# Sums of weight quarters: by accumulating DMAs, instead of on GpSimd, in a decoder's MLP

## The chip, the cores and the metric

The program runs on one core of a Trainium2 chip, in one launch. The metric is the device time of the launch in microseconds, the median of several runs. The engines are TensorE (PE; PEld is its weight load), VectorE (DVE), ScalarE (ACT), GpSimd (POOL) and SyncE (SP), which here only issues DMAs. Sixteen DMA engines serve the core.

## The reference

A trunk of two layers, on 512 tokens of width 1024, all in float32. Layer 0 is a stick-breaking attention, layer 1 a gated linear recurrence (HGRN2); a squared-ReLU MLP of width 4096 follows each. Only the MLP matters here.

```python
def squared_relu_mlp(h, w1, w2):
    a = jax.nn.relu(h @ w1)
    return (a * a) @ w2

def reference(...):
    for layer in range(DEPTH):
        ...
        h = rmsnorm(x, norm_gains[layer, 1])
        x = x + squared_relu_mlp(h, mlp_w1[layer], mlp_w2[layer])
    return x
```

## The kernel before

**Numbers.** A float32 product is made of three products of a shorter format: every operand is split into a rounded part (`hi`, made by ScalarE as a cast) and the rest (`lo`, made by VectorE or GpSimd as operand minus `hi`), and TensorE forms hi·hi, hi·lo and lo·hi into the same PSUM buffer. So each weight tile costs one ScalarE cast and one subtraction before TensorE can use it. The split halves of a slab of weights are `wh` and `wl`, two buffers each: while TensorE works with one slab, the next is split.

**The MLP** goes in four rounds per layer, eight in all. A round `q` takes 1024 of the 4096 hidden columns.

1. Four slabs of `mlp_w1`, 256 columns each, two chains of 24 matmuls per slab (`gemm_w`). Each chain gives 128 hidden rows for 512 tokens in PSUM (tag `mm`, two buffers). VectorE empties it into `u` (ReLU and norm factor), ScalarE squares `u`, and `Seven.take` makes from it the left operands of the second matrix. The first four chunks give A11 and A21 (`raw_a`, split as `a11`); with the last four come A12 and A22 (`a`, split as `a2h`, `a2l`) and the sums S3 and S1 (`s31h`, `s31l`), S4 and S2 (`s42h`, `s42l`).
2. The second matrix is done as a 2 x 2 block product with seven block products instead of eight (`seven_products`): A is tokens by hidden columns, cut in the middle of both; B is the 1024 x 1024 piece of `mlp_w2`, cut into quarters B11, B12, B21, B22. Each quarter is two tiles of 128 x 1024 (512 KB each), named `raw`. The right operands are B11, B21, B22 and four sums: T1 = B12 - B11, T2 = B22 - T1, T3 = B22 - B12, T4 = B21 - T2. The sums are made in place in the quarters' tiles (`minus`). A block product is two chains of 12 matmuls, one per 128 tokens. Its PSUM buffers come from tag `mm` for the first, third, fifth and seventh product, from tag `z` (two buffers) for the others.
3. Each product is added to the residual stream `xt[0]`, `xt[1]` (left and right 512 columns, four token tiles each) by `back`, on VectorE straight from PSUM. A running sum `U` of the products a11, s2 and s3 is added to three blocks of `xt` by GpSimd.

**What sets the order.** The code is written as generators; `line` deals out TensorE's work, whose order is fixed by hand. The other engines' order is chosen by a scheduler from the program's order and its own estimates; each engine then executes its instructions strictly in the order chosen, waiting at each for its operands and buffers. `Weights.next` hands TensorE a slab and at once prepares the next one of the plan: loads (`load`), then the split (`slab`). Loads of B's quarters stand in the plan between the four slabs of `mlp_w1`.

Of the kernel before, what the change touches and what calls it, by code (L numbers as in the profile page):

```python
# [13 lines left out]
ALU = mybir.AluOpType  # L14
AX = mybir.AxisListType

P = 128
D = 1024
S = 512
# [40 lines left out]
def trunk(  # L60
# [17 lines left out]
    nc = tc.nc  # L78
# [20 lines left out]
    def f(t):  # L99
        return t.bitcast(F32)  # L100
# [71 lines left out]
    rows = sb("AT", (40, P), name="rows")  # L172
# [97 lines left out]

    def quarters(w, r0):

        got = {}

        def load(i, j):
            tag = {(0, 0): "B", (1, 0): "X5", (0, 1): "R4", (1, 1): "R4"}[i, j]
            shape = (P, 10 * P) if tag == "X5" else (P, TT, SLAB)
            got[i, j] = []
            for a in range(2):
                t = sb(tag, shape, name="raw")  # L280
                t = t if tag == "X5" else t.rearrange("p t c -> p (t c)")
                t = t[:, : 2 * S].rearrange("p (k c) -> p k c", c=S)
                r = r0 + i * (D // 2) + a * 2 * P
                nc.sync.dma_start(
                    out=t, in_=w[r : r + 2 * P, j * S : (j + 1) * S].rearrange("(k p) c -> p k c", p=P)
                )
                got[i, j].append(t)

        return got, load

    def minus(eng, o, x, y):
        for a in range(2):
            eng.tensor_tensor(out=o[a], in0=x[a], in1=y[a], op=ALU.subtract)  # L293

    def seven(w, r0):

        b, load = quarters(w, r0)

        def slab(src, eng=nc.vector):
            hi = wp.tile([P, KT // 2, S], F32R, tag="wh", bufs=2, name="wh")  # L300
            lo = wp.tile([P, KT // 2, S], F32R, tag="wl", bufs=2, name="wl")
            for a in range(2):
                c = slice(2 * a, 2 * a + 2)
                nc.scalar.copy(hi[:, c, :], src[a])  # L304
                eng.tensor_tensor(out=lo[:, c, :], in0=src[a], in1=f(hi[:, c, :]), op=ALU.subtract)  # L305
            return hi, lo

        def b11():
            got = slab(b[0, 0])
            minus(nc.gpsimd, b[0, 0], b[0, 1], b[0, 0])  # L310
            minus(nc.gpsimd, b[0, 1], b[1, 1], b[0, 1])
            return got

        def t1():
            got = slab(b[0, 0])
            minus(nc.vector, b[0, 0], b[1, 1], b[0, 0])
            return got

        def t2():
            got = slab(b[0, 0])  # L320
            minus(nc.gpsimd, b[1, 0], b[1, 0], b[0, 0])
            return got

        loads = [lambda at=at: load(*at) for at in ((0, 0), (0, 1), (1, 1), (1, 0))]
# [375 lines left out]

    def back(h, t, p, eng=nc.vector):
        eng.tensor_tensor(out=xt[h][:, t, :], in0=xt[h][:, t, :], in1=p, op=ALU.add)  # L702

# [42 lines left out]
    class Seven:  # L746
# [5 lines left out]
        def take(self, u):  # L752

            A, B = slice(0, S // 2), slice(S // 2, S)
            k = len(self.raw)
            if k < 4:
# [12 lines left out]
            nc.scalar.activation(out=a, in_=u, func=AF.Square)  # L769
            nc.gpsimd.tensor_tensor(out=raw[:, B], in0=raw[:, B], in1=a[:, B], op=ALU.add)  # L770
            self.a2.append(self.two_parts(a, "Q", "a2"))
            nc.vector.tensor_tensor(out=a[:, B], in0=a[:, B], in1=raw[:, A], op=ALU.subtract)
            nc.vector.tensor_tensor(out=a[:, A], in0=a[:, A], in1=a[:, B], op=ALU.subtract)  # L773
            self.s31.append(self.two_parts(raw, "qT", "s31"))
            self.s42.append(self.two_parts(a, "Q" if k < 2 else "qT", "s42"))
# [14 lines left out]

    def seven_products(A, done):

# [11 lines left out]

        def p5(t, p):
            back(1, t, p)
            back(1, 2 + t, p)

        def p6(t, p):
            nc.vector.tensor_add(U[t], U[t], p)  # L810
            back(1, t, U[t], nc.gpsimd)

        def p3(t, p):
            back(1, t, p)
            done(1, t)

        def p7(t, p):
            nc.vector.tensor_add(U[t], U[t], p)
            back(1, 2 + t, U[t], nc.gpsimd)
            back(0, 2 + t, U[t], nc.gpsimd)  # L820
            done(1, 2 + t)

        def p4(t, p):
            back(0, 2 + t, p)
# [12 lines left out]
    def mlp(norm, nxt=None):  # L837
        task = line.spawn(norm.finish())
        rounds = FF // D
        for q in range(rounds):  # L840
# [29 lines left out]

            yield from seven_products(A, done)

# [369 lines left out]
```

## Time and profile before

| | |
|---|---|
| median of 3 runs | 1418.32 us (1418.27 to 1420.58) |
| profiled execution | 1418.27 us, its span 1416.5 us |
| TensorE busy | 1303.9 us, 92% of the span |
| VectorE, ScalarE, GpSimd busy | 1007.0, 566.1, 419.8 us |
| mean granted TensorE clock | 0.966 |
| moved by DMA | 110.67 MB |
| attention with its projection | 0 to about 317 us |
| first MLP | 317 to 711 us |
| recurrence with its projection | 711 to 1018 us |
| second MLP | 1018 to 1416 us |

A row of the profile's groups of instructions reads: line, engine, operation, output from inputs, partitions x elements of each, count, busy time in all, mean ns of one, idle time of the engine before it and what ended that. Matmuls overlap: their durations are longer than the distance from one to the next. A wait is put down to the instruction that ended last before the waiter went on, which need not be the one that was waited for.

### The profile page before, as it was taken

How to read it: one execution, taken by the hardware profiler on the slowest of the kernel's cores; microseconds unless marked ns; L12 is line 12 of the kernel's file. 1: busy time of each engine (PE TensorE's matmuls, PEld its weight loads, DVE VectorE, ACT ScalarE, POOL GpSimd, SP SyncE). 2: the span in 40 equal slices, each digit the busy share in tenths (PEclk: the TensorE clock that was granted, in tenths of full speed). 3: DMA queues.
4: the chain of work that ended last, by engine and by line, in shares of the span. 5: the costliest groups of instructions: out<-in, count | busy, mean ns of one | idle time of the engine just before them, and what ended most of it. 6: DMA issues, size and time to landing. Idle time of an engine off the chain costs nothing. (4 is left out here: it accounts for less than half of the span.)

```text
span 1416.5 us, 17879 instructions
## 1 busy us (share of the span) xinstructions
PE 1303.9 (92%) x6817; PEld 1088.8 (77%) x6817; DVE 1007.0 (71%) x1671; ACT 566.1 (40%) x943; POOL 419.8 (30%) x331
## 2 busy tenths in 40 slices
PE   8999999999798898898889999999997988988987
PEld 7988988788577676676678888888875776766765
DVE  4887687765856757757778879796667677578575
ACT  5545364444333434334343333332433333343341
POOL 1000000003624524525513223130045245255154
PEclk9999999999899999999999999999998998999998
DMA  6211123131141141240022212134211412413201
GB/s 176 91 60 53 38 90 105 47 117 61 33 146 60 60 149 30 102 130 6 14 81 65 82 60 72 55 113 149 90 60 58 137 43 69 139 31 119 74 12 49
DMA packets 91190, 110.67 MB, mean 78 GB/s; under 512 B 3832, under 2 KB 69536, under 8 KB 91104
## 3 DMA queue, kind: packets, MB, share of 16 engines
q1 hardware_dynamic: 91024, 109.22, 24.2%
q8 instruction: 54, 0.88, 0.3%
q0 software_dynamic: 80, 0.31, 0.1%
q14 instruction: 32, 0.26, 0.1%
HBM read 107.41 MB, written 2.10 MB: 77 GB/s over the span
## 5 line engine op out<-in xcount | busy, mean ns | idle before, releaser
L154 PE MATMUL ps_mm<-xh,wh 128*128 128x512 f32 x592 | 232.6, 393 | 5.9 <-DVE xt L702 5.9
L154 PE MATMUL ps_mm<-xh,wl 128*128 128x512 f32 x592 | 230.5, 389 | 0.0
L154 PE MATMUL ps_mm<-xl,wh 128*128 128x512 f32 x592 | 230.4, 389 | 0.0
L267 DVE TENSOR_TENSOR wl<-wr,wh 128x1024 fp32r<-128x1024 f32 x134 | 177.9, 1346 | 14.2 <-ACT wh L266 13.7
L266 ACT CAST wh<-wr 128x1024 fp32r<-128x1024 f32 x134 | 136.4, 1052 | 122.9 <-PE ps_mm L154 117.8
L154 PE MATMUL ps_mm<-wh,xh 128*128 128x256 f32 x592 | 173.6, 293 | 0.0
L154 PE MATMUL ps_mm<-wl,xh 128*128 128x256 f32 x592 | 167.9, 284 | 1.3 <-DVE wl L536 1.3
L304 ACT CAST wh<-raw 128x1024 fp32r<-128x1024 f32 x112 | 112.0, 1047 | 141.3 <-PE ps_mm L154 120.5
L154 PE MATMUL ps_mm<-wh,xl 128*128 128x256 f32 x592 | 167.8, 283 | 0.0
L293 POOL TENSOR_TENSOR raw<-raw 128x1024 f32<-128x1024 f32 x48 | 132.4, 2766 | 105.0 <-DVE raw L293 61.5
L154 PEld LDWEIGHTS ps_mm<-xh,wh 128*128 128x128 f32 x592 | 111.2, 188 | 30.6 <-issue 8.3
L154 PEld LDWEIGHTS ps_mm<-xh,wl 128*128 128x128 f32 x592 | 111.1, 188 | 23.5
L154 PEld LDWEIGHTS ps_mm<-xl,wh 128*128 128x128 f32 x592 | 111.2, 188 | 22.2
L764 POOL TENSOR_TENSOR raw_a<-raw_a 128x256 f32<-128x256 f32 x32 | 23.6, 739 | 352.6 <-DVE a L763 237.1
L154 PEld LDWEIGHTS ps_mm<-wh,xh 128*128 128x128 f32 x592 | 113.5, 192 | 4.2 <-issue 3.6
L154 PEld LDWEIGHTS ps_mm<-wl,xh 128*128 128x128 f32 x592 | 113.7, 192 | 2.1 <-DVE wl L536 1.5
L305 DVE TENSOR_TENSOR wl<-raw,wh 128x1024 fp32r<-128x1024 f32 x80 | 109.6, 1402 | 6.5 <-ACT wh L304 6.5
L154 PEld LDWEIGHTS ps_mm<-wh,xl 128*128 128x128 f32 x592 | 113.7, 192 | 0.0
L702 DVE TENSOR_TENSOR xt<-xt,ps_mm 128x512 f32<-128x512 f32 x128 | 85.1, 678 | 34.6 <-PE ps_mm L154 34.4
L854 DVE SCALAR_TENSOR_TENSOR u<-ps_mm,R 128x512 f32<-128x512 f32 x60 | 41.3, 688 | 90.7 <-PE ps_mm L154 90.7
L305 POOL TENSOR_TENSOR wl<-raw,wh 128x1024 fp32r<-128x1024 f32 x32 | 90.7, 2855 | 30.8 <-ACT wh L304 30.8
L154 PE MATMUL ps_mm<-wh,a 128*128 128x512 f32 x128 | 56.3, 507 | 38.9 <-ACT s42h L779 35.5
(234 smaller groups left out, 2750.3 us busy)
## 6 DMA issues: line engine op xcount, KB each, us to landing
raw<-in_mlp_w_dram SPq DMA_DIRECT2D x64, 512.0 KB, 3.6
wr<-in_mlp_w_dram SPq DMA_DIRECT2D x64, 512.0 KB, 3.8
wr<-in_hg_w_in_dram SPq DMA_DIRECT2D x32, 512.0 KB, 3.7
wr<-in_sb_w_qkv_dram SPq DMA_DIRECT2D x22, 512.0 KB, 3.7
wr<-in_sb_w_o_dram SPq DMA_DIRECT2D x8, 512.0 KB, 4.2
wr<-in_hg_w_o_dram SPq DMA_DIRECT2D x8, 512.0 KB, 3.8
xt<-in_x_dram SPq DMA_DIRECT2D x8, 256.0 KB, 6.0
out_dram<-xt SPq DMA_DIRECT2D x8, 256.0 KB, 2.0
```

The source lines that it names most:

```text
L154: nc.tensor.matmul(o, lhsT=lhsT, rhs=rhs, start=start, stop=stop, **kw)
L266: nc.scalar.copy(hi[:, c, :], raw)
L267: nc.vector.tensor_tensor(out=lo[:, c, :], in0=raw, in1=f(hi[:, c, :]), op=ALU.subtract)
L293: eng.tensor_tensor(out=o[a], in0=x[a], in1=y[a], op=ALU.subtract)
L304: nc.scalar.copy(hi[:, c, :], src[a])
L305: eng.tensor_tensor(out=lo[:, c, :], in0=src[a], in1=f(hi[:, c, :]), op=ALU.subtract)
L702: eng.tensor_tensor(out=xt[h][:, t, :], in0=xt[h][:, t, :], in1=p, op=ALU.add)
L764: nc.gpsimd.tensor_tensor(out=raw[:, A], in0=raw[:, A], in1=raw[:, B], op=ALU.subtract)
L854: nc.vector.scalar_tensor_tensor(out=u, in0=p, scalar=0.0, in1=norm.R, op0=ALU.max, op1=ALU.mult)
```

## The change

Four things change, all in the MLP.

1. A sum of two quarters is no longer a subtraction on GpSimd or VectorE. ScalarE negates the target in place (`flip`), and a DMA that GpSimd issues adds the other quarter onto it (`accum_op=ALU.add`), either from the weights in HBM or from the other quarter's tile. The tile of B12 becomes B11 - B12, that is -T1, then with B22 from HBM T2; the tile of B11 becomes T2 - B11 = T3; the tile of B21 becomes T2 - B21 = -T4. The products with -T1 and -T4 are subtracted from `xt`. That makes eight accumulating transfers of 512 KB and six negations a round.
2. All slabs are split by ScalarE and VectorE; the two that GpSimd took go to VectorE. So do the two sums per chunk in `Seven.take` that GpSimd made.
3. `U` is added to `xt` by accumulating DMAs of 256 KB, six a round, except in the last round of a layer, where VectorE does it.
4. The order of the products: a11, s1, a12, s4, s2, s3, a22 instead of a11, a12, s1, s2, s4, s3, a22. The quarters' loads come in the order B12, B11, B22, B21 instead of B11, B12, B22, B21.

```diff
+        def flip(at, plus):
+            for a in range(2):
+                nc.scalar.mul(b[at][a], b[at][a], -1.0)
+                nc.gpsimd.dma_start(out=b[at][a], in_=plus(a), accum_op=ALU.add)
...
+        def t1():
+            flip((0, 1), lambda a: rows(0, 0, a))
+            load(1, 1)
...
+        def slab_t1():
+            got = slab((0, 1))
+            for a in range(2):
+                nc.gpsimd.dma_start(out=b[0, 1][a], in_=rows(1, 1, a), accum_op=ALU.add)
+            flip((0, 0), lambda a: b[0, 1][a])
             return got
 
-        def t2():
-            got = slab(b[0, 0])
-            minus(nc.gpsimd, b[1, 0], b[1, 0], b[0, 0])
+        def slab_b21():
+            got = slab((1, 0))
+            flip((1, 0), lambda a: b[0, 1][a])
             return got
...
         slabs = [
-            b11, lambda: slab(b[1, 0], nc.gpsimd), t1, t2, lambda: slab(b[1, 1], nc.gpsimd),
-            lambda: slab(b[0, 1]), lambda: slab(b[1, 0]),
+            lambda: slab((0, 0)), slab_t1, slab_b21, lambda: slab((1, 1)), lambda: slab((0, 1)),
+            lambda: slab((0, 0)), lambda: slab((1, 0)),
         ]
-        return [("load", g) for g in loads], [("slab", g) for g in slabs]
+        return [("load", g) for g in (b12, b11, t1, b21)], [("slab", g) for g in slabs]
...
-                nc.gpsimd.tensor_tensor(out=raw[:, A], in0=raw[:, A], in1=raw[:, B], op=ALU.subtract)
+                nc.vector.tensor_tensor(out=raw[:, A], in0=raw[:, A], in1=raw[:, B], op=ALU.subtract)
...
-            nc.gpsimd.tensor_tensor(out=raw[:, B], in0=raw[:, B], in1=a[:, B], op=ALU.add)
+            nc.vector.tensor_tensor(out=raw[:, B], in0=raw[:, B], in1=a[:, B], op=ALU.add)
             self.a2.append(self.two_parts(a, "Q", "a2"))
+            self.s31.append(self.two_parts(raw, "qT", "s31"))
...
+        def add(h, t, u):
+            if last:
+                back(h, t, u)
+            else:
+                nc.gpsimd.dma_start(out=xt[h][:, t, :], in_=u, accum_op=ALU.add)
...
         def p7(t, p):
             nc.vector.tensor_add(U[t], U[t], p)
-            back(1, 2 + t, U[t], nc.gpsimd)
-            back(0, 2 + t, U[t], nc.gpsimd)
+            add(1, 2 + t, U[t])
             done(1, 2 + t)
+            add(0, 2 + t, U[t])
...
         steps = [
-            ("a11", p1), ("a12", p2), ("s1", p5), ("s2", p6), ("s4", p3), ("s3", p7), ("a22", p4),
+            ("a11", p1), ("s1", p5), ("a12", p2), ("s4", p3), ("s2", p6), ("s3", p7), ("a22", p4),
         ]
```

In the changed kernel the cast of `slab` is line 302 (before: 304), its subtraction 303 (305), the negation 294, the accumulating transfers 295 and 324, those of `U` 824, `back` 710 (702), `u` 868 (854), the halves of `two_parts` 787 and 788 (779, 780), the sums in `take` 772, 778, 781 and 782 (764, 770, 772, 773).

GpSimd in the first round, before (the rounds are alike). The numbers behind the names tell the tiles apart: `raw_3399` and `raw_3401` are the two tiles of B11, `raw_3553` and `raw_3555` of B12, `raw_3633` and `raw_3635` of B22, `raw_3735` and `raw_3737` of B21.

```order
L770 TENSOR_TENSOR raw_a_3539<-raw_a_3539,a_3674 128x256
L293 TENSOR_TENSOR raw_3399<-raw_3553,raw_3399 128x1024
L770 TENSOR_TENSOR raw_a_3547<-raw_a_3547,a_3718 128x256
L293 TENSOR_TENSOR raw_3553<-raw_3633,raw_3553 128x1024
L293 TENSOR_TENSOR raw_3401<-raw_3555,raw_3401 128x1024
L293 TENSOR_TENSOR raw_3555<-raw_3635,raw_3555 128x1024
L770 TENSOR_TENSOR raw_a_3594<-raw_a_3594,a_3776 128x256
L305 TENSOR_TENSOR wl_3838<-raw_3735,wh_3837 128x1024
L305 TENSOR_TENSOR wl_3838<-raw_3737,wh_3837 128x1024
```

GpSimd in the second round, after (`raw_4101` and `raw_4103` are the tiles of B12, `raw_4181` and `raw_4183` of B11, `raw_4367` and `raw_4369` of B21, `raw_4729` and `raw_4731` those of the third round's B12).

```order
L324 DMA raw_4101<-in_mlp_w2_dram 128x2x512
L324 DMA raw_4103<-in_mlp_w2_dram 128x2x512
L295 DMA raw_4181<-raw_4101 128x1024
L295 DMA raw_4183<-raw_4103 128x1024
L295 DMA raw_4367<-raw_4101 128x1024
L295 DMA raw_4369<-raw_4103 128x1024
L295 DMA raw_4729<-in_mlp_w2_dram 128x2x512
L295 DMA raw_4731<-in_mlp_w2_dram 128x2x512
L824 DMA xt1_100<-U_4490 128x512
L824 DMA xt1_100<-U_4506 128x512
L824 DMA xt1_100<-U_4490 128x512
L824 DMA xt0_99<-U_4490 128x512
```

The queue holds transfers only, and the next round's first pair stands ahead of this round's sums of `U`.

VectorE where the first matrix of the second round ends, before: from the `u` of the chunk that is third from the end to that of the last.

```order
L854 SCALAR_TENSOR_TENSOR u<-ps_mm,R 128x512
L305 TENSOR_TENSOR wl<-raw,wh 128x1024 x2
L780 TENSOR_TENSOR a2l<-a,a2h 128x512
L772 TENSOR_TENSOR a<-a,raw_a 128x256
L780 TENSOR_TENSOR s31l<-raw_a,s31h 128x512
L773 TENSOR_TENSOR a<-a 128x256
L854 SCALAR_TENSOR_TENSOR u<-ps_mm,R 128x512
L780 TENSOR_TENSOR s42l<-a,s42h 128x512
```

The same place after:

```order
L868 SCALAR_TENSOR_TENSOR u<-ps_mm,R 128x512
L303 TENSOR_TENSOR wl<-raw,wh 128x1024 x2
L778 TENSOR_TENSOR raw_a<-raw_a,a 128x256
L788 TENSOR_TENSOR a2l<-a,a2h 128x512
L788 TENSOR_TENSOR s31l<-raw_a,s31h 128x512
L781 TENSOR_TENSOR a<-a,raw_a 128x256
L782 TENSOR_TENSOR a<-a 128x256
L868 SCALAR_TENSOR_TENSOR u<-ps_mm,R 128x512
L788 TENSOR_TENSOR s42l<-a,s42h 128x512
```

The sum that GpSimd made stands on VectorE (L778), and `u` stands at the same place behind the chunk before it.

VectorE at the end of the same round, with what each waits for, after (DMASW is a transfer that GpSimd issued, DMAHW one that SyncE issued):

```order
L832 TENSOR_TENSOR U<-U,ps_mm 128x512 [waits DMASW1_49,DVE_49,PE_49]
L832 TENSOR_TENSOR U<-U,ps_mm 128x512 [waits DMASW2_49,DVE_49,PE_49]
L267 TENSOR_TENSOR wl<-wr,wh 128x1024 [waits DMAHW7_49,Activation_49]
L267 TENSOR_TENSOR wl<-wr,wh 128x1024 [waits DMAHW0_49,Activation_49]
L710 TENSOR_TENSOR xt_99<-xt_99,ps_mm 128x512 [waits DMASW4_49,PE_49]
L710 TENSOR_TENSOR xt_99<-xt_99,ps_mm 128x512 [waits DMASW6_49,PE_49]
```

Before, the same instructions waited for GpSimd's arithmetic or for nothing but TensorE (`[waits PE_49,Pool_49]` at the last, `[waits DVE_49,PE_49]` at `U`). Now the second sum into `U` waits until the transfer that reads `U` is done, and the last sums into `xt` until the transfers onto them have landed; the split of the next slab of `mlp_w1` (L267) stands between.

More of the change, by code (lines that the diff above doesn't have):

```diff
@@ L269, in slab_halves, with seven, rows @@
         return hi, lo, load, split
-    def quarters(w, r0):
-        got = {}
+    def seven(w, r0):
+        b = {}
+        def rows(i, j, a):
+            r = r0 + i * (D // 2) + a * 2 * P
+            return w[r : r + 2 * P, j * S : (j + 1) * S].rearrange("(k p) c -> p k c", p=P)
         def load(i, j):
@@ L282, in load, with slab @@
                 t = t[:, : 2 * S].rearrange("p (k c) -> p k c", c=S)
[L283 to L299, printed above, removed]
+                nc.sync.dma_start(out=t, in_=rows(i, j, a))
+                b[i, j].append(t)
+        def flip(at, plus):
+            for a in range(2):
+                nc.scalar.mul(b[at][a], b[at][a], -1.0)
+                nc.gpsimd.dma_start(out=b[at][a], in_=plus(a), accum_op=ALU.add)
+        def slab(at):
             hi = wp.tile([P, KT // 2, S], F32R, tag="wh", bufs=2, name="wh")
@@ L698, in head, with back @@
             outs[slot] = split_out(shared["po"])
-    def back(h, t, p, eng=nc.vector):
-        eng.tensor_tensor(out=xt[h][:, t, :], in0=xt[h][:, t, :], in1=p, op=ALU.add)
+    def back(h, t, p, op=ALU.add):
+        nc.vector.tensor_tensor(out=xt[h][:, t, :], in0=xt[h][:, t, :], in1=p, op=op)
     def chain(o, wsl, acts):
@@ L789, in part, with seven_products @@
             return [[blk(x, at + t) for x in pair] for pair in src]
-    def seven_products(A, done):
+    def seven_products(A, done, last):
         U = []
@@ L805, in p5, with p3 @@
         def p5(t, p):
+            back(1, t, p, ALU.subtract)
+            back(1, 2 + t, p, ALU.subtract)
+        def p3(t, p):
             back(1, t, p)
-            back(1, 2 + t, p)
+        def add(h, t, u):
[3 more added lines that the diff above has]
+                nc.gpsimd.dma_start(out=xt[h][:, t, :], in_=u, accum_op=ALU.add)
         def p6(t, p):
             nc.vector.tensor_add(U[t], U[t], p)
-            back(1, t, U[t], nc.gpsimd)
-        def p3(t, p):
-            back(1, t, p)
+            add(1, t, U[t])
             done(1, t)
@@ L869, in done @@
                     nxt.turn(h, LAG["x7"] if h else LAG["x"])
-            yield from seven_products(A, done)
+            yield from seven_products(A, done, q == rounds - 1)
     def hgrn(norm):
```

24 lines of the change are left out of this document (11 added, 13 removed).

## Prediction

> **What bounds the kernel now.** I read the page first, then the waits of TensorE, then one round of the MLP instruction by instruction. The first part of the page, and TensorE's waits (total us, times, longest):
>
> ```profile
> PE 1303.9 (92%) x6817; PEld 1088.8 (77%) x6817; DVE 1007.0 (71%) x1671; ACT 566.1 (40%) x943; POOL 419.8 (30%) x331
> ...
> PE ps_mm L154 <- ACT s42h L779: 35.5, 8, 4.4
> PE ps_mm L154 <- DVE wl L305: 26.9, 16, 1.8
> PE ps_mm L154 <- DVE s42l L780: 10.9, 8, 1.6
> PE ps_mm L154 <- DVE xt L702: 6.9, 7, 1.0
> ```
>
> TensorE is the bound, and its four longest waits come 7, 8 or 16 times in eight MLP rounds: they are one pattern, repeated. The timeline of TensorE in the second round (start, duration, what stood before) and the stretches' busy times (us, PE busy, its count, then PEld, DVE, ACT, POOL, the granted clock, DMA share, GB/s) give its price.
>
> ```profile
> 459.12 0.77 PE L154 MATMUL ps_mm<-wh,a 128*128 128x512 f32 x1 [4.44 <-ACT s42h L779]
> 459.69 0.63 PE L154 MATMUL ps_mm<-wl,a 128*128 128x512 f32 x1
> 467.50 0.39 PE L154 MATMUL ps_mm<-wh,a2h 128*128 128x512 f32 x1
> 473.57 0.40 PE L154 MATMUL ps_mm<-wh,s31h 128*128 128x512 f32 x1
> 479.16 0.40 PE L154 MATMUL ps_mm<-wh,s42h 128*128 128x512 f32 x1
> 497.69 0.40 PE L154 MATMUL ps_mm<-wh,s31h 128*128 128x512 f32 x1
> 503.28 0.40 PE L154 MATMUL ps_mm<-wh,a2h 128*128 128x512 f32 x1
> 509.91 0.47 PE L154 MATMUL ps_mm<-xh,wh 128*128 128x512 f32 x1 [0.99 <-DVE xt L702]
> 558.17 0.76 PE L154 MATMUL ps_mm<-wh,a 128*128 128x512 f32 x1 [4.45 <-ACT s42h L779]
> ```
> ```profile
> 411.00:455.00 44.00, 43.68 (x192) 35.83 (x192) 25.48 (x27) 15.28 (x22) 12.69 (x9) 1.00 0.27 84
> 455.00:510.00 55.00, 44.28 (x169) 33.92 (x170) 41.44 (x43) 21.17 (x26) 29.95 (x16) 0.91 0.26 86
> ```
>
> A round lasts 558.17 - 459.12 = 99.05 us. Undisturbed, its first-matrix part takes 43.7 us (192 matmuls, clock 1.00), so each of its eight chains 5.46; one product takes 503.28 - 497.69 = 5.59 us, seven 39.1. So 82.8 us of work and 16.25 us lost: 4.44 ahead of a11; 8.38 - 5.59 = 2.8 inside a11, whose matmuls start at 0.63 instead of 0.39 us each, so a wait of this length is paid again in a lower clock; 0.5 in a12; 18.53 - 11.18 = 7.35 in s2 and s4; 1.04 at the end. Who makes TensorE wait is seen on VectorE and GpSimd:
>
> ```profile
> 444.11 0.69 DVE L854 SCALAR_TENSOR_TENSOR u<-ps_mm,R 128x512 f32<-128x512 f32 x1
> ...
> 450.50 2.60 DVE L772 TENSOR_TENSOR a<-a,raw_a 128x256 f32<-128x256 f32 x1 [0.63 <-POOL raw_a L770]
> 453.03 2.87 DVE L780 TENSOR_TENSOR s31l<-raw_a,s31h 128x512 fp32r<-128x512 f32 x1
> 455.82 2.56 DVE L773 TENSOR_TENSOR a<-a 128x256 f32<-128x256 f32 x1
> 458.30 0.68 DVE L854 SCALAR_TENSOR_TENSOR u<-ps_mm,R 128x512 f32<-128x512 f32 x1
> 461.14 0.69 DVE L780 TENSOR_TENSOR s31l<-raw_a,s31h 128x512 fp32r<-128x512 f32 x1
> 461.75 0.42 DVE L772 TENSOR_TENSOR a<-a,raw_a 128x256 f32<-128x256 f32 x1
> 450.43 7.67 POOL L293 TENSOR_TENSOR raw<-raw 128x1024 f32<-128x1024 f32 x3
> 482.40 2.22 DVE L305 TENSOR_TENSOR wl<-raw,wh 128x1024 fp32r<-128x1024 f32 x1
> 485.74 1.66 DVE L780 TENSOR_TENSOR s42l<-a,s42h 128x512 fp32r<-128x512 f32 x1
> ```
>
> The same L772 takes 0.42 us alone and 2.60 while GpSimd runs its three L293; s31l 0.69 against 2.87. Behind them stands u at 458.30, which empties the PSUM buffer that a11 needs. The wait is booked on s42h, but u ended at 458.98, just before the matmul at 459.12: it is VectorE's backlog. In s2 and s4 it is the same: wl 2.22 us, s42l 1.66.
>
> **The change part by part.** First the prices: durations of a line (least/median/greatest ns), transfers with the us from issue to landing, GpSimd's own issue of one (start, duration), and two more stretches.
>
> ```profile
> L305 DVE TENSOR_TENSOR wl<-raw,wh x80: 1211/1219/2223, 345.7 to 1403.9; 128x1024 fp32r<-128x1024 f32 x80
> L304 ACT CAST wh<-raw x112: 1030/1047/1057, 344.6 to 1402.7; 128x1024 fp32r<-128x1024 f32 x112
> L779 ACT CAST a2h<-a 128x512 fp32r<-128x512 f32 x32 | 19.9, 622 | 1.0
> raw<-in_mlp_w_dram SPq DMA_DIRECT2D x64, 512.0 KB, 3.6
> out_dram<-xt SPq DMA_DIRECT2D x8, 256.0 KB, 2.0
> 2.40 0.71 POOL L206 DMA_DIRECT2D masks_i<-in_level_masks_dram  x1
> masks_i<-in_level_masks_dram POOLq DMA_DIRECT2D x1, 300.0 KB, 5.7
> 481.00:502.00 21.00, 17.42 (x66) 13.45 (x67) 15.22 (x16) 6.13 (x7) 11.16 (x5) 0.92 0.47 155
> 455.00:481.00 26.00, 19.85 (x73) 15.03 (x73) 20.10 (x23) 12.01 (x17) 12.77 (x8) 0.87 0.00 0
> ```
>
> *GpSimd's arithmetic goes.* VectorE falls back to 0.42, 0.69 and 1.22 us.
>
> *VectorE takes on,* per round, four slab halves (4 x 1.22 = 4.9) and eight 256-wide sums (8 x 0.42 = 3.4), and loses two L293 (2.4 at the undisturbed price). Its whole round becomes: eleven slabs 22 x 1.22 = 26.8; eight u 5.5; four first-half chunks 4 x 0.84; four second-half chunks 4 x 3.33 (u left out); 16 PSUM evacuations in the products at 0.69, 11.0. Sum 60 of 82.8 us. It fits on average; tight is the second half of the first matrix, four chunks with u (16.1) and two slabs (4.9), 21.0 us in four chains, 21.8 us. So I walk it in the new order. TensorE's last two chains end at 449.2 and 454.7 (410.9 + 43.7); an instruction of VectorE follows the one before by its duration less 0.08 (461.14 to 461.75), and a hop to ScalarE costs its 0.62. From u at 444.11, as now: slab one's halves to 447.1; the sum 447.5; a2l, after ScalarE has made a negation, the square and the copy, 448.5; s31l 449.1; two differences 449.9; u of the chunk before last 450.6; s42l 451.3; then the same list for that chunk: 451.6, 452.5, 453.1, 453.9, s42l 455.2; u of the last chunk 455.9. a11 needs these two buffers at 454.7 and 457.5. Then T1's halves 457.0 and 458.1 (s1 starts at 460.3), sum 458.5, xt 459.1, a2l 459.7, s31l 460.3, needed as s1's fourth operand near 462.4. Nothing waits, and the least margin is 1.6 us. So the 4.44 and the 2.8 go.
>
> *The new order* puts s1 second and s4, s2 fourth and fifth. The last s42l, late for s2 by 1.4 us now (10.9 / 8), ends about 466 for a use at 471.4. Slab by slab VectorE finishes 464.2, 470.5, 474.7, 480.4 and 485.9 for products that start at 465.9, 471.4, 477.0, 482.6 and 488.1: the 7.35 go, with 0.9 us as least margin.
>
> *ScalarE takes on* six negations per round at 1.05 (the L304 row, same shape): 6.3 us on an engine busy 21 of 55. Two stand ahead of copies that TensorE needs: those of the next round's B12 wait for their load, behind them the copies of the sixth slab. The load is issued when slab four is split (470.5), lands 3.6 us later, so the second negation ends by 475.6; the copies wait for TensorE until 477.0 anyway. Cost nothing; if the load were 2 us later, it begins to cost. SP's queue issues the same loads in another order, and each row of it has the buffer's last reader to wait for, as now.
>
> *GpSimd's queue* issues 14 accumulating transfers a round, 14 x 0.71 = 10 us against 12.7 + 30.0 us of arithmetic. What is queued behind a wait there: the six U sums behind the two transfers for the next round's B12.
>
> *The transfers themselves* are not in this trace. Eight of 512 KB and six of 256 KB a round. Their DMA time: let p be what 512 KB occupy. The stretch 481 to 502 moved 155 GB/s at a share of 0.47, 330 GB/s at full share, so a plain one takes 1.6 us: the lower end. The upper end is the row of the only transfer in GpSimd's queue, 300 KB in 5.7 us, as if all of it were occupation: 9.7 us. What does p cost? The first can start when T1's first half is split (457.0 + 0.71), and DMA is idle there now (share 0.00); the U sum that the last evacuation of xt waits for must land by 493.0, since TensorE's next first-matrix chain needs that PSUM buffer at 493.7. In these 35.2 us DMA also carries eight loads (12.8): 22.4 us are left for 8 p + 4 (p/2) = 10 p. So nothing waits up to p = 2.2; beyond, each round of the six that sum by DMA loses 10 (p - 2.2) + 2.8 us, the 2.8 again for the clock. I take p between 1.6 and 2.2, nearest to the plain row, since both are the same 16 engines and the 5.7 was taken at the start, with all first loads under way. Latency alone: two issues after U's add (486.5) make 487.9, so 5.1 us are left to land; plain 256 KB take 2.0, twice that 4.0.
>
> The Trainium skill (Collectives: The Full Stack, "The bandwidth ceiling") says that an adding transfer reads two sources through one ring and so runs at half a copy's rate, 31 / 2 GB/s per engine. An estimate from its figures is 248 GB/s over 16 engines, p = 2.1, which leaves the sum as it is. No run here shows it yet.
>
> *The last round of each layer* sums U on VectorE: six more evacuations, 4.1 us, in a stretch where it is busy 28 of 39 by the count above.
>
> **Sum.** Eight rounds lose 8 x 16.25 = 130 us. I keep 1.5 us a round for what the walk cannot see (the 0.5 us that a12 loses now, a margin of 1 us at the round's end): 12. The profiled execution was 1418.27 us (span 1416.5 and 1.8 around it), its own median 1418.32: 1418.3 - 130 + 12 = 1300.
>
> **Rivals.**
> 1. *Accumulation at half rate.* Each byte added has to be read from two places. On this trace's own rate p = 3.2; DMA is then full from 458 on, the U sums land late, VectorE stands at its U and xt instructions, and TensorE waits 10 x 1.0 + 2.8 = 12.8 us in each of six rounds: 1300 + 77 = 1377. For it: the second read must happen. Against it: SBUF sources may be quicker than the loads from which 330 GB/s comes. The Trainium skill's rule above would bring exactly this.
> 2. *Slower.* The same mechanism decides against the change from 10 (p - 2.2) + 2.8 = 118 / 6 = 19.7 us, p = 3.9, 2.4 times a plain transfer. At p = 5 it is 1300 + 6 x 30.8 = 1485, at the upper bound of 9.7 it would be 1767. For it: the 5.7 us of the GpSimd queue's row, and the bunch of transfers in 38 us of every round. Against it: nothing in the trace needs more than two reads.
> 3. *GpSimd still disturbs VectorE,* when it builds transfers: 14 x 0.71 = 10 us of VectorE a round, mostly in its 22 idle us; at the round's end two issues lie in the path, about 1.4 us, and some slab margins of 0.9 break, 2 us: 1300 + 8 x 2 = 1316. The masks row was taken with VectorE idle and cannot tell.
> 4. *No effect,* were VectorE's slow instructions not GpSimd's doing. The same instruction at 0.42 and 2.60 us speaks against it.
>
> **How the numbers follow.** Forecast (1288 to 1316) 0.50; rival 1 in all its sizes, p from 2.2 to 3.9, 0.30; rival 2 0.10; rival 3 0.07; rival 4 0.03. The low end, 1285, is all 130 us and a little; the high end, 1385, takes in rival 1 up to p = 3.3 and leaves out its rest (0.05), rivals 2 and 4: some 0.18. Within 0.2%, which is about what a measurement of this kernel can tell from no change, lies rival 4 alone: 0.03. Slower 0.10, faster 0.87.
>
> **What the profile after would show.** Right: a11 following the last first-matrix chain without a wait, a round of 83 to 85 us, L772's and L780's later lines at 0.42 and 0.69 throughout, PEclk 1.00 in the products, POOL with no arithmetic in the MLP. Wrong: TensorE waiting at the first chain of a round, VectorE idle ahead of U or xt with a DMA as releaser (rivals 1 and 2, and p is read from the queue's share), or a11 still waiting for u (the walk was wrong).

## The result, and the profile after

The changed kernel takes 1343.89 us (median of three runs, 1343.56 to 1345.82) where the kernel before took 1418.32: the ratio is 0.9474, with a 95% interval from 0.9453 to 0.9496. The profiled execution has a span of 1341.9 us. The forecast was 1300 with a range of 1285 to 1385: the gain is there, 44 us smaller than the likeliest case had it.

Busy times from the page, TensorE's longest waits in the MLP, and VectorE's waits for the `U` transfers (total us, times, longest):

```profile
PE 1273.8 (95%) x6817; PEld 1079.9 (80%) x6817; DVE 933.5 (70%) x1763; ACT 611.6 (46%) x991; POOL 178.4 (13%) x239
...
PE ps_mm L154 <- DVE xt L710: 36.5, 7, 7.3
...
PE ps_mm L154 <- DVE wl L303: 4.2, 6, 0.8
...
PE ps_mm L154 <- ACT wh L302: 2.0, 4, 0.9
...
DVE U L832 <- DMA xt<-U: 38.5, 12, 5.8
...
DVE xt L710 <- DMA xt<-U: 35.6, 12, 4.7
```

The waits for `s42h` and `s42l` are gone, that for `wl` fell from 26.9 to 4.2 us; that for `xt` grew from 6.9 to 36.5, and VectorE in turn stands at the U transfers. TensorE's second round shows where: the first matmuls of the products, and of the next round's first matrix.

```profile
449.28 0.39 PE L154 MATMUL ps_mm<-wh,a 128*128 128x512 f32 x1
454.73 0.40 PE L154 MATMUL ps_mm<-wh,s31h 128*128 128x512 f32 x1
460.32 0.39 PE L154 MATMUL ps_mm<-wh,a2h 128*128 128x512 f32 x1
465.77 0.39 PE L154 MATMUL ps_mm<-wh,s42h 128*128 128x512 f32 x1
477.53 0.49 PE L154 MATMUL ps_mm<-wh,s31h 128*128 128x512 f32 x1 [0.53 <-ACT wh L302]
478.79 0.50 PE L154 MATMUL ps_mm<-wl,s31h 128*128 128x512 f32 x1 [0.77 <-DVE wl L303]
484.24 0.39 PE L154 MATMUL ps_mm<-wh,a2h 128*128 128x512 f32 x1
494.56 0.76 PE L154 MATMUL ps_mm<-xh,wh 128*128 128x512 f32 x1 [4.72 <-DVE xt L710]
540.73 0.39 PE L154 MATMUL ps_mm<-wh,a 128*128 128x512 f32 x1
```

a11, s1, a12, s4 and s2 now follow each other in 5.45 to 5.59 us with no wait. The round lasts 540.73 - 449.28 = 91.45 us instead of 99.05. What is still lost stands late in it: some 1.8 us at s3, 4.72 at the next first matrix, and about 2.5 in that matrix, which takes 46.17 us instead of the 43.7 of before, at a granted clock of 0.94. VectorE at the end of the round, and the three stretches by busy time (us, PE, PEld, DVE, ACT, POOL, the granted clock, DMA share, GB/s):

```profile
487.27 0.69 DVE L832 TENSOR_TENSOR U<-U,ps_mm 128x512 f32<-128x512 f32 x1 [3.94 <-DMA xt<-U]
489.16 0.69 DVE L832 TENSOR_TENSOR U<-U,ps_mm 128x512 f32<-128x512 f32 x1 [1.20 <-DMA xt<-U]
489.77 2.35 DVE L267 TENSOR_TENSOR wl<-wr,wh 128x1024 fp32r<-128x1024 f32 x2
493.73 0.69 DVE L710 TENSOR_TENSOR xt<-xt,ps_mm 128x512 f32<-128x512 f32 x1 [1.61 <-DMA xt<-U]
499.10 0.69 DVE L710 TENSOR_TENSOR xt<-xt,ps_mm 128x512 f32<-128x512 f32 x1 [4.69 <-DMA xt<-U]
```
```profile
449.28:454.73 5.45, 5.45 (x26) 4.51 (x25) 5.45 (x8) 4.24 (x6) 2.44 (x2) 1.00 0.13 15
454.73:494.56 39.83, 33.81 (x146) 26.85 (x144) 24.32 (x30) 17.96 (x19) 11.18 (x12) 0.98 1.07 241
494.56:540.73 46.17, 46.17 (x192) 37.98 (x193) 26.66 (x42) 19.89 (x30) 0.00 (x0) 0.94 0.32 98
```

The 16 DMA engines are full (share 1.07) from the second product to the end of the round, and move only 241 GB/s. The queues show which transfers take the time (packets, MB, share of 16 engines' span; then transfers and their median us to landing):

```profile
q1 hardware_dynamic: 91024, 109.22, 25.1%
q0 software_dynamic: 18576, 43.31, 18.4%
...
raw<-in_mlp_w_dram SPq DMA_DIRECT2D x64, 512.0 KB, 7.5
wr<-in_mlp_w_dram SPq DMA_DIRECT2D x64, 512.0 KB, 4.7
...
xt<-U POOLq DMA_DIRECT2D x36, 256.0 KB, 6.0
```

GpSimd's queue, which holds the accumulating transfers, takes 18.4% of the engines' time for 43.31 MB: 175 GB/s at full share, 3.0 us for 512 KB. SP's plain loads have 109.22 MB in 25.1%: 324 GB/s, 1.6 us. The quarter loads, which landed in 3.6 us before, now take 7.5.

### The profile page after: what moved, and what is told of

It is laid out like the page before. It is cut to its first block, busy times and chain, and to the rows that moved or that the text cites. A ratio compares the mean times of both kernels' runs of the same rounds, so it can differ in the third digit from the quotient of the medians.

```text
span 1341.9 us, 17978 instructions
## 1 busy us (share of the span) xinstructions
PE 1273.8 (95%) x6817; PEld 1079.9 (80%) x6817; DVE 933.5 (70%) x1763; ACT 611.6 (46%) x991; POOL 178.4 (13%) x239
## 3 DMA queue, kind: packets, MB, share of 16 engines
q1 hardware_dynamic: 91024, 109.22, 25.1%
q0 software_dynamic: 18576, 43.31, 18.4%
## 5 line engine op out<-in xcount | busy, mean ns | idle before, releaser
L154 PE MATMUL ps_mm<-xh,wh 128*128 128x512 f32 x592 | 237.9, 402 | 35.5 <-DVE xt L710 35.5
L154 PE MATMUL ps_mm<-xl,wh 128*128 128x512 f32 x592 | 235.2, 397 | 0.0
L154 PE MATMUL ps_mm<-xh,wl 128*128 128x512 f32 x592 | 235.1, 397 | 0.0
L267 DVE TENSOR_TENSOR wl<-wr,wh 128x1024 fp32r<-128x1024 f32 x134 | 162.1, 1231 | 9.1 <-ACT wh L266 8.9
L154 PEld LDWEIGHTS ps_mm<-xh,wh 128*128 128x128 f32 x592 | 114.5, 193 | 61.4 <-issue 37.9
L303 DVE TENSOR_TENSOR wl<-raw,wh 128x1024 fp32r<-128x1024 f32 x112 | 132.7, 1220 | 37.4 <-ACT wh L302 37.3
L324 POOL DMA_DIRECT2D raw<-in_mlp_w_dram x16 | 19.5, 1247 | 546.5 <-DVE wl L303 546.0
L294 ACT ACTIVATE raw<-raw 128x1024 f32<-128x1024 f32 x48 | 50.7, 1059 | 38.7 <-DMA raw<-in_mlp_w_dram 38.7
L667 DVE TENSOR_TENSOR_SCAN sn<-sn,later 128x128 f32<-128x128 f32 (+3 forms) x64 | 51.2, 816 | 8.4 <-ACT sn L664 7.4
L154 PE MATMUL ps_mm<-wl,s31h 128*128 128x512 f32 x128 | 51.7, 404 | 4.2 <-DVE wl L303 4.2
```

Of the source, the lines that this page charges most:

```text
L154: nc.tensor.matmul(o, lhsT=lhsT, rhs=rhs, start=start, stop=stop, **kw)
L267: nc.vector.tensor_tensor(out=lo[:, c, :], in0=raw, in1=f(hi[:, c, :]), op=ALU.subtract)
L294: nc.scalar.mul(b[at][a], b[at][a], -1.0)
L303: nc.vector.tensor_tensor(out=lo[:, c, :], in0=b[at][a], in1=f(hi[:, c, :]), op=ALU.subtract)
L324: nc.gpsimd.dma_start(out=b[0, 1][a], in_=rows(1, 1, a), accum_op=ALU.add)
L667: nc.vector.tensor_tensor_scan(out=rev, data0=rev, data1=later[:, S - W :][:, ::-1], initial=1.0, op0=ALU.mult, op1=ALU.max,)
```

## Experiments

The theory: GpSimd's arithmetic was the loss, as forecast; what is missing was given back because accumulating transfers occupy the DMA engines nearly twice as long as plain ones, fill the product phase, and so the `U` sums (and less so the load for the next T1) land late. The rivals: GpSimd's issuing, the U sum's own trip, and, for the gain, the order of the products.

**U on VectorE in every round.**

```diff
-            yield from seven_products(A, done, q == rounds - 1)
+            yield from seven_products(A, done, True)
```

> The changed kernel with the U sums on VectorE in all eight rounds (as already in each layer's last round), so that six transfers of 256 KB a round are gone. Theory, late U sums: the six rounds lose their wait of 4.7 to 7.3 us at the next round's first chain and about 2 us of slow clock behind it, some 8 us each; VectorE takes on 6 x 0.69 = 4.1 us a round. 1343.9 - 48 = 1296 us (1288 to 1305); about 1 us a round stays at s3, since the eight quarter sums still delay the next round's load. Rival, the waits belong to the load of the next round's weights (the first chain waits for VectorE, and VectorE could as well stand at a weight slab that landed late): no more than 15 us are won, 1330 us or above.

Measured: 1295.56 us, ratio to the kernel before 0.9136 (0.9118 to 0.9154). A round takes 84.8 us; TensorE's wait at the round's start is 0.66 us and the first matrix behind it 43.64. The rival that put the wait on the next weights falls: 48 us hang on the U sums. The 1.2 us at s3 stay, as expected.

**All transfers plain.**

```diff
-                nc.gpsimd.dma_start(out=b[at][a], in_=plus(a), accum_op=ALU.add)
+                nc.gpsimd.dma_start(out=b[at][a], in_=plus(a))
...
-                nc.gpsimd.dma_start(out=xt[h][:, t, :], in_=u, accum_op=ALU.add)
+                nc.gpsimd.dma_start(out=xt[h][:, t, :], in_=u)
```

> The changed kernel with all its accumulating transfers made plain ones, same tiles, same queue, same waits; the additions are left out. Theory, half rate: a plain 512 KB occupies 1.6 us instead of 3.0, the product phase carries 10 x 1.6 + 12.8 = 29 us of transfers in 35 us, VectorE no longer stands at U and xt, the load of the next B12 lands in about 4 us: 1300 us (1292 to 1310), waits at a round's first chain under 1 us. Rival, GpSimd's issuing (14 transfers at 0.9 to 1.2 us each, in order): nothing changes, 1340 us (1333 to 1345).

Measured: 1284.95 us, ratio 0.906 (0.9044 to 0.9077), below the expected range. This kernel leaves the additions out, so only its time counts. The same bytes in the same queue take half the time (its row in this run):

```profile
q0 software_dynamic: 12176, 43.31, 9.6%
```

9.6% of 1283.4 us, 351 GB/s. GpSimd still issues all 14 transfers of a round, in the same order, but each issue is shorter (medians 0.54 to 0.73 us against 0.93 to 1.21), so this run alone does not clear the issuing. The changed kernel's own trace does: the two `U` transfers for which VectorE stands until 487.27 and 489.16 had both been issued by 482.54.

**Only U plain.** The edit is the last pair of lines above, alone.

> Only the six U transfers of a round made plain; the quarter sums stay accumulating, the additions of U are left out. Theory, half rate on the whole queue: the phase still carries 8 x 3.0 + 4 x 0.8 + 12.8 = 40 us in 35 us, against 43 before, so about 3 us of the wait go in each of six rounds: 1326 us (1315 to 1333). Rival, the U sums' own trip (read, add, write back) is what is late: the waits go altogether, 1300 us. Rival, GpSimd's issuing: 1340 us.

Measured: 1325.05 us, ratio 0.9337 (0.9318 to 0.9355), within 1 us of the first theory's number. The longest wait at the round's start falls to 4.7 us, its total from 36.5 to 22.4. So 19 of the 48 us that hang on the `U` transfers go when these are plain; the rest stays, and is owed to what else is in the queue, since with the quarter sums plain too it goes.

**The transfers alone.** One kernel of nothing but transfers, in blocks of eight; `d` are eight tiles of 512 KB, `e` eight sources in SBUF.

```python
def load_add(n):
    nc.gpsimd.dma_start(out=three(d[n]), in_=rows(n), accum_op=ALU.add)
...
def move_add(n):
    nc.gpsimd.dma_start(out=d[n], in_=e[n], accum_op=ALU.add)
```

> Transfers alone, nothing beside them, none of the reference computed: eight of 512 KB each, back to back, from memory in SP's queue, from memory in GpSimd's, the same accumulating, from SBUF plain, from SBUF accumulating, the two accumulating kinds once more, and then 256 KB ones and 512 KB ones chained on one tile. Theory, half rate: a plain one occupies 1.6 us (about 330 GB/s), an accumulating one about 3.0 us (about 175 GB/s) from either source; a chained 256 KB sum takes 3.5 to 4 us from issue to landing, a plain one 2 to 2.5. Rival, issuing: both kinds at the same bandwidth at full share, eight of them spaced by 0.9 to 1.25 us of GpSimd.

Windows of that run, each with one kind of transfer in it (us, DVE, POOL, clock, DMA share, GB/s): plain loads from memory (SP's and GpSimd's), accumulating from memory, plain from SBUF, accumulating from SBUF, and accumulating from memory once more. The second block from SBUF runs beside SP's writes of the output and is left out.

```profile
6.00:15.00 9.00, 7.54 (x10) 2.34 (x3) 1.00 0.99 325
35.00:46.00 11.00, 0.00 (x0) 1.02 (x1) 1.00 1.13 206
52.00:57.00 5.00, 0.00 (x0) 2.53 (x5) 1.00 0.92 356
60.00:75.00 15.00, 0.00 (x0) 6.05 (x7) 1.00 1.05 202
85.00:100.00 15.00, 0.00 (x0) 6.37 (x6) 1.00 1.11 197
```

Plain: 325 GB/s from memory, 356 at a share of 0.92 from SBUF. Accumulating: 206 and 197 from memory, 202 from SBUF, with the engines full. So 512 KB take 2.5 to 2.7 us alone, a little less than the 3.0 expected, against 1.6 plain; among the kernel's other loads they take 3.0. Chained on one tile, GpSimd issues a new 256 KB transfer every 2.6 us plain and every 3.5 us accumulating:

```profile
133.72 0.54 POOL L116 DMA_DIRECT2D d<-e x1 [2.04 <-DMA d<-e]
136.28 0.54 POOL L116 DMA_DIRECT2D d<-e x1 [2.02 <-DMA d<-e]
...
142.43 0.85 POOL L118 DMA_DIRECT2D d<-e x1 [2.74 <-DMA d<-e]
145.97 0.84 POOL L118 DMA_DIRECT2D d<-e x1 [2.70 <-DMA d<-e]
```

A `U` sum's own round trip, issue included, is 3.5 us, against 6.0 in the kernel; by this measure the difference is owed to the other transfers in its way.

**Quarter sums on VectorE, U by transfers.**

```diff
-                nc.scalar.mul(b[at][a], b[at][a], -1.0)
-                nc.gpsimd.dma_start(out=b[at][a], in_=plus(a), accum_op=ALU.add)
+                nc.vector.tensor_tensor(out=b[at][a], in0=plus[a], in1=b[at][a], op=ALU.subtract)
```

(and T2's two sums as VectorE additions)

> The changed kernel with the eight quarter sums of a round on VectorE (one subtraction or addition of 128x1024 each, no negation on ScalarE), the U sums still by accumulating transfers. Theory, a full queue: U's six transfers of 1.5 us and 12.8 us of loads are 22 us in 35 us, so a U sum lands 3 to 4 us after its issue, and the wait at a round's first chain falls from 5 to 7 us to 0 to 2; VectorE has 60 + 9.8 = 70 of 82.8 us to do: 1303 us (1294 to 1315). Rival, the trip of a U sum itself, with GpSimd's issue of four in a row: the waits stay, 1335 us or above.

Measured: 1336.76 us, ratio 0.9432 (0.9412 to 0.9452): a miss of 34 us, at the rival's number. With the load of a round spread evenly the queue should have had room. It is not spread: SP issues five quarter loads between 476.7 and 483.3, as their buffers come free late in the round, and the U sums fall among them. Four stretches at the round's end, and the U transfers' row:

```profile
480.00:484.00 4.00, 3.71 (x17) 2.84 (x16) 2.75 (x3) 0.71 (x1) 0.51 (x1) 1.00 1.06 268
484.00:488.00 4.00, 4.00 (x19) 3.28 (x18) 2.39 (x3) 2.01 (x2) 1.77 (x2) 1.00 1.06 352
488.00:490.00 2.00, 2.00 (x10) 1.50 (x8) 2.00 (x3) 0.00 (x0) 1.50 (x2) 1.00 1.12 294
490.00:492.00 2.00, 0.23 (x2) 0.00 (x0) 0.48 (x1) 1.04 (x1) 0.27 (x1) 1.00 1.12 212
...
xt<-U POOLq DMA_DIRECT2D x36, 256.0 KB, 7.1
```

The engines are full here too and a `U` sum lands in 7.1 us. This run does not tell the queue from the trip, which was the rival; the 3.5 us measured alone speak for the queue. On that reading what failed is the average over 35 us, in the expectation and in the prediction's 10 p against 22.4 us alike: the queue must be counted where the transfers bunch.

**All sums on VectorE.** Both edits together.

> The changed kernel with quarter sums and U sums on VectorE in every round: no accumulating transfer, no GpSimd in the MLP at all. VectorE has 60 + 9.8 + 4.1 = 74 of 82.8 us a round to do. Theory (GpSimd's arithmetic was the loss, VectorE has the room): 1303 us (1293 to 1315). Rival, VectorE becomes late where its work is dense (second half of the first matrix, products two to five): TensorE waits 3 to 5 us a round for slabs and s42l, 1325 to 1340 us.

Measured: 1316.64 us, ratio 0.9297 (0.9275 to 0.9319): 21 us above the run with `U` alone on VectorE, just over the expected range and short of the rival's. TensorE's longest wait is now VectorE's own backlog, at s3:

```profile
PE ps_mm L154 <- DVE wl L302: 18.7, 8, 2.6
```

VectorE has the room on average and, in this row, not where it is needed; the eight quarter sums of a round are worth their transfers, as long as U is not among them.

**The kernel before with its arithmetic on VectorE.** All of GpSimd's sums and splits in the MLP are moved, nothing else.

```diff
-            minus(nc.gpsimd, b[0, 0], b[0, 1], b[0, 0])
-            minus(nc.gpsimd, b[0, 1], b[1, 1], b[0, 1])
+            minus(nc.vector, b[0, 0], b[0, 1], b[0, 0])
+            minus(nc.vector, b[0, 1], b[1, 1], b[0, 1])
...
```

> The kernel before, old order of the seven products, with all of GpSimd's arithmetic in the MLP moved to VectorE and nothing else. Theory (GpSimd's arithmetic stretched VectorE's instructions): VectorE's two-input instructions fall to 0.42, 0.69 and 1.22 us throughout, the waits at a11 go (7.2 us a round), those in s2 and s4 mostly: 1310 us (1300 to 1325). Rival, the order of the products carries a good part: s2 and s4 keep 4 to 7 us a round, 1335 to 1355 us. Rival, GpSimd did not disturb: VectorE only gets more work, 1418 us or above.

Measured: 1361.48 us, ratio 0.9613 (0.9588 to 0.9637), outside all three ranges. VectorE's two-input instructions fall to 0.42, 0.68 and 1.22 us throughout, and a11, s2 and s4 wait for nothing: that part holds. One new wait takes 7.65 us a round, and with the slow clock behind it (0.78 in this product) a12 takes 15.39 us, the wait included, instead of 5.45:

```profile
PE ps_mm L154 <- DVE wl L305: 61.2, 8, 7.7
```

In VectorE's row three quarter sums (L293, 455.69 to 459.1 us in the second round) and an `s42l` stand ahead of the second half of the split of B21's slab, which ends at 460.9; a12 goes on at 460.97.

**The same with T1's and T3's sums placed later,** behind the splits of the slabs for B21 and B22.

```diff
         def b11():
-            got = slab(b[0, 0])
-            minus(nc.vector, b[0, 0], b[0, 1], b[0, 0])
-            minus(nc.vector, b[0, 1], b[1, 1], b[0, 1])
-            return got
+            return slab(b[0, 0])
+
+        def b21():
+            got = slab(b[1, 0])
+            minus(nc.vector, b[0, 0], b[0, 1], b[0, 0])
+            return got
...
```

> The kernel before, old order of the seven products, all its sums on VectorE, but T1's placed behind the split of B21's slab and T3's behind the split of B22's, instead of all four behind the first slab. Theory: the 7.65 us at a12 in the run with the sums at their old place came from VectorE's own row of quarter sums ahead of B21's split, not from the order of the products; with the sums later they shrink to under 2 us: 1300 us (1290 to 1318). Rival, the old order itself is late, whatever stands where, since T1's sum and two more slabs are then due within two products: 1345 us or above.

Measured: 1350.23 us, ratio 0.9523 (0.9507 to 0.9539): a miss. a12 waits 0.64 us instead of 7.65, but s1 now waits 5.10 for `s31l`, which stands in VectorE's row behind the sums that T1 and T2 want within two products. The wait moved. With all sums on VectorE the new order is 34 us faster (1316.64); how much of this is the order itself and how much the row that the scheduler made of it these two runs do not tell apart.

**The kernel before with only the six quarter subtractions moved to VectorE.**

> The kernel before with only the six 128x1024 quarter subtractions that stood on GpSimd moved to VectorE; the splits of two slabs, the 256-wide sums and the U sums stay on GpSimd. Theory: the stretch around a11 is made by these subtractions, so its 4.4 + 2.8 us a round go and s2 and s4 keep their 7 us: 1418.3 - 8 x 7.2 = 1361 us (1345 to 1380). Rival, any GpSimd arithmetic beside VectorE costs as much (the 256-wide sums and the slab splits too): less than 25 us are won, 1393 us or above.

Measured: 1392.44 us, ratio 0.9825 (0.9807 to 0.9843): a miss by 31 us, on the rival's side. a11 still loses 3.9 us, s2 and s4 together 8.8. The splits on GpSimd (L305) now meet the same VectorE instructions:

```profile
452.79 5.43 POOL L305 TENSOR_TENSOR wl<-raw,wh 128x1024 fp32r<-128x1024 f32 x2 [2.44 <-ACT wh L304]
453.38 2.60 DVE L772 TENSOR_TENSOR a<-a,raw_a 128x256 f32<-128x256 f32 x1
455.90 0.68 DVE L854 SCALAR_TENSOR_TENSOR u<-ps_mm,R 128x512 f32<-128x512 f32 x1
456.50 1.99 DVE L773 TENSOR_TENSOR a<-a 128x256 f32<-128x256 f32 x1
```

The first L305 runs from 452.79 to 455.69; VectorE's L772, 0.42 us when alone, started behind it and ends at 455.98, 0.29 after it. L773, begun beside the second L305 (455.64 to 458.22), ends 0.28 after that one. `u`, which reads PSUM, runs at its usual 0.68 beside the second. The Trainium skill (SBUF — State Buffer, "Who interferes with whom") says that VectorE and GpSimd share one pair of ports under an exclusive lock, and that a VectorE instruction with two SBUF inputs contends with a GpSimd instruction that reads SBUF; by that rule this row is what one would see, and the trace agrees.

**The small sums back on GpSimd.** From the kernel with U on VectorE, L772 and L778 alone.

```diff
-                nc.vector.tensor_tensor(out=raw[:, A], in0=raw[:, A], in1=raw[:, B], op=ALU.subtract)
+                nc.gpsimd.tensor_tensor(out=raw[:, A], in0=raw[:, A], in1=raw[:, B], op=ALU.subtract)
...
-            nc.vector.tensor_tensor(out=raw[:, B], in0=raw[:, B], in1=a[:, B], op=ALU.add)
+            nc.gpsimd.tensor_tensor(out=raw[:, B], in0=raw[:, B], in1=a[:, B], op=ALU.add)
```

> The kernel with the U sums on VectorE, and the sixteen 256-wide sums and differences of a round that the change took from GpSimd (L772 and L778, eight a round, 0.74 and 0.85 to 1.1 us each there) put back on it; nothing else differs, the transfers stay. Theory, GpSimd's arithmetic stretches VectorE's two-input instructions beside it: in the second half of the first matrix VectorE's 256-wide differences and splits go from 0.42 and 0.69 to 0.9 us and more, u comes late, a11 waits and runs at a slow clock, as in the run that kept them (3.9 us a round): 1310 us (1298 to 1328). Rival, only long GpSimd instructions disturb: 1296 us, VectorE's durations as without.

Measured: 1300.78 us, ratio 0.9177 (0.9159 to 0.9195), 5.2 us slower than without. Only `a2l`, which starts beside L778, is stretched (least, median, greatest ns):

```profile
L788 DVE TENSOR_TENSOR a2l<-a,a2h x32: 692/746/1782, 341.7 to 1259.5; 128x512 fp32r<-128x512 f32 x32
L788 DVE TENSOR_TENSOR s31l<-raw_a,s31h x32: 677/693/694, 342.6 to 1262.2; 128x512 fp32r<-128x512 f32 x32
```

a11 does not wait. The 5 us stand at s3, where TensorE's waits for `wh` and `wl` grow from 5.6 to 8.5 us in all; how the short sums bring that about these runs do not show. So GpSimd's short sums (0.74 and 1.02 us on average here) cost little in this kernel. By elimination the loss of before goes with the longer ones, quarter sums and splits of 2.8 us and `U` sums of 1.45 us each; the `U` sums were not tried apart from the others.

**T4 on VectorE as well as U.**

```diff
-            flip((1, 0), lambda a: b[0, 1][a])
+            for a in range(2):
+                nc.vector.tensor_tensor(
+                    out=b[1, 0][a], in0=b[0, 1][a], in1=b[1, 0][a], op=ALU.subtract
+                )
```

> The kernel with the U sums on VectorE, and the two sums for T4 on it as well (one subtraction each, no negation); T1, T2 and T3 stay accumulating transfers. Theory: T1's load for the next round must wait until the transfers for T4 have read T2; without these two (some 6 us of transfer) it lands before ScalarE reaches its negation, and the 1.2 us at s3 and most of the 0.7 us at the round's start go: 1295.6 - 8 x 1.2 = 1286 us (1282 to 1291). Rival: VectorE, in order, now stands at T4 until the transfer for T2 has landed, and the last s42l and the slab of B21 behind it come late: 1296 us or above.

Measured: 1297.87 us, ratio 0.9153 (0.9137 to 0.917), as without. Half of the theory held: the loads' median landing fell from 6.9 to 5.0 us, ScalarE's wait for them at the negations from 35.6 to 6.0 us in all, and the waits at s3 and at the round's start are gone (a round 84.05 us instead of 84.83). The reason given was not right: the load's buffers come free with the slab of B22, not with T2's last reader (SP issues it at 452.57, when the first half of that split has just ended, at 452.54). It was late, then, because T4's transfers were in the queue before it. And one new wait ate the gain:

```profile
PE ps_mm L154 <- DVE s42l L791: 12.9, 8, 1.6
```

Not for VectorE standing at T4, as the rival had it: the scheduler had put the last `s42l` behind T4's sums and four more slab halves, at 458.36 instead of 450.61 us in the two runs.

**And the split of s42 ahead.**

```diff
-            self.s42.append(self.two_parts(a, "Q" if k < 2 else "qT", "s42"))
+            with tc.high_priority(offset=20):
+                self.s42.append(self.two_parts(a, "Q" if k < 2 else "qT", "s42"))
```

> The run with U and T4 on VectorE, and the last split of s42 given a higher priority, so that it stands behind the first half of the third slab again, ahead of three more slab halves and the two T4 sums. Theory: the 1.6 us a round at s42l (12.9 us in all) were only its place in VectorE's row; they go, and nothing else is late, since the load for the next T1 now lands in time: 1297.9 - 12.9 = 1285 us (1281 to 1291), as fast as the run in which all transfers were plain. Rival, VectorE has no room left there: the slab of B22 or of T2 comes late in place of s42l, 1293 us or above.

Measured: 1282.03 us (1281.47 to 1283.49), ratio 0.9036 (0.9018 to 0.9055), the fastest here: 4.6% under the changed kernel. In its second round TensorE has no wait in the MLP, and the round takes 82.15 us. Its longest wait overall is now one of the recurrence between the two MLPs:

```profile
PE 1254.6 (98%) x6817; PEld 1070.1 (84%) x6817; DVE 975.6 (76%) x1815; ACT 596.3 (47%) x975; POOL 132.5 (10%) x187
...
PE ps_s L154 <- DVE sc L1034: 6.7, 16, 0.7
```

## Why the prediction came out as it did

*The loss and its cause* (16.25 us a round from GpSimd's arithmetic): right. The fastest run has 99.05 - 82.15 = 16.9 us less in each of eight rounds, 135 us, and ends at 1282; the step said 130. That run changes more than GpSimd's arithmetic, and the runs that move the arithmetic alone give VectorE more to do, so none of them shows the whole 16.25 by itself; that GpSimd stretched VectorE's instructions, and that a11 waited for this, they do show. VectorE's prices fell as named, in the changed kernel too:

```profile
L781 DVE TENSOR_TENSOR a<-a,raw_a x32: 411/418/422, 344.1 to 1304.9; 128x256 f32<-128x256 f32 x32
```

*The walk of VectorE through the second half*: right. a11 waits for nothing, and s4 and s2 find their slabs; `u` of the last chunk, which the walk had done 1.2 us behind the end of the first matrix, was done 1.21 behind it (450.49 against 449.28).

*The price of a transfer* is the step that failed. p was taken at 1.6 to 2.2, "nearest to the plain row, since both are the same 16 engines"; it is 3.0 in the kernel. That both kinds run on the same engines did not settle how long a byte occupies them. Rival 1, at 0.30, is what happened, with its place (`U`, `xt`, TensorE at the round's start) as described, and the range held only because it took this rival in. At p = 3.0 its formula gives 10.8 us in each of six rounds; these rounds are 92.15 us on average, 10.0 above the 82.15 that the work takes, so 60 us in all, and 1282 + 60 = 1342. Its own total, 1300 + 65 = 1365, is 21 too high, nearly all of it from the base: the 12 us kept for what the walk could not see were not needed, and a round's work was put at 82.8 instead of 82.15. The formula itself came close although it counts evenly what comes in bunches, leaves out the wait at s3, and takes the slow clock for 2.8 where the six first matrices lost 1.6 to 2.5. That is partly luck: the same even count missed by 34 us with the quarter sums on VectorE.

The Trainium skill's halving rule (Collectives: The Full Stack, "The bandwidth ceiling") is stated there for the reduce step of a ring between cores. Its ratio is borne out roughly: in the kernel the same transfers go at 351 GB/s plain and 175 adding, SP's loads at 324; alone it is 325 to 206 from memory, a factor of 1.6. That a second read is the reason no run here shows. Its figure for an engine is not borne out: the estimate of 248 GB/s from it, p = 2.1, was above all that was measured (175 to 206), and so kept the sum as it was.

*ScalarE's negations*: the condition came true. "If the load were 2 us later, it begins to cost": the two loads of the next B12 land 9.9 and 10.3 us after their issue (463.01 to 472.88 and 465.10 to 475.40), where 3.6 was reckoned. ScalarE stands at the negations, the copies behind them begin late, and s3 pays about 1.8 us:

```profile
472.96 1.06 ACT L294 ACTIVATE raw<-raw 128x1024 f32<-128x1024 f32 x1 [4.99 <-DMA raw<-in_mlp_w_dram]
475.48 1.06 ACT L294 ACTIVATE raw<-raw 128x1024 f32<-128x1024 f32 x1 [1.46 <-DMA raw<-in_mlp_w_dram]
476.45 3.87 ACT L302 CAST wh<-raw 128x1024 fp32r<-128x1024 f32 x4
```

*GpSimd's issues* were taken at 0.71; the accumulating ones take 0.93 to 1.21 us by their medians. No wait of TensorE was traced back to this: the `U` transfers at the round's end were issued in time, and in the fastest run TensorE waits for nothing in the MLP with six of them left in a round. *Rival 3* (issuing disturbs VectorE) falls: L781 never exceeds 0.422 us, `s42l` 0.694.

*The new order* was given the 7.35 us in s2 and s4. In the kernel before, with GpSimd quiet and the old order, these are gone as well, which speaks for GpSimd as their cause. It does not show it: in both runs of that kind an earlier wait of the same round (7.65 us at a12, 5.10 at s1) gave VectorE time to catch up. What the order is worth was seen only together with other rows of VectorE (34 us).

## What to carry to other kernels

Moving work from an engine to accumulating transfers turns its time into bandwidth: count each added byte at about half the plain rate, and count it in the stretch where the buffers come free and the transfers bunch, not over the phase. Keep from them what the next stage waits for directly (here U), and let them have what is needed a product or two later. After each wait that goes, look at the row of the engine that is next: twice here the gain was held back by one short instruction standing behind work that could wait.

## What was not expected of the hardware

An accumulating transfer runs as fast from SBUF as from memory (202 against 197 to 206 GB/s, alone), while GpSimd needs longer to issue it from memory (1.2 us) than from SBUF (0.85), and less for a plain one (0.54 to 0.87).

What a wait of TensorE costs in clock behind it does not grow with its length. Behind waits of up to 0.68 us a first matrix takes 43.5 to 43.6 us. Behind waits of 2.69 to 7.26 us it takes either 45.1 to 45.6 or 46.1 to 46.5: with the quarter sums on VectorE the same 3.95 us were followed by 46.48 in one round and by 45.25 in the next, and in the changed kernel 4.72 by 46.17 and 7.26 by 45.49. The records of the granted clock show a stretch at 0.50 with each of these waits, of 6.8 us (it can begin within the wait) or of 3.4. With all sums on VectorE 2.62 us at s3 brought such a stretch of 3.4 us in the first round and none in the second.
